# Feed-forward blocks by seven products: four products gathered in one PSUM bank, weights split two quarters at a time

## The chip, the cores and the metric

One core of a Trainium2 chip runs the whole program. Its engines are TensorE (PE, matrix products; its weight loads are shown apart as PEld), VectorE (DVE), ScalarE (ACT), GpSimd (POOL) and SyncE (SP, which here only issues DMAs). Each engine works through a list of instructions of its own, in order, and waits where an instruction needs something that another engine or a DMA has not finished. Products land in PSUM, in banks of 128x512 floats; everything else that is computed lies in SBUF.

The metric is the device time of one execution in microseconds (us). Three executions of the kernel before took 2611.4, 2611.07 and 2610.01 us, median 2611.07 us. One more was taken with the profiler: it took 2612.16 us, and its span from the first to the last instruction is 2610.0 us.

## The reference

Two layers of an encoder over 640 rows (512 new frames and 8 x 16 running ones) of width 1024. Each layer is a feed-forward block, a mixer and a second feed-forward block, and each of the six has a residual and a layer norm behind it:

```python
D_MODEL = 1024
D_FF = 2816

def swiglu(x, w_gate, w_up, w_down):
    return (jax.nn.silu(x @ w_gate) * (x @ w_up)) @ w_down

def trunk(x, states):
    for l in range(DEPTH):
        x = layer_norm(ALPHA * x + 0.5 * swiglu(x, ffn_w_gate[l, 0], ffn_w_up[l, 0], ffn_w_down[l, 0]),
                       ln_g[l, 0], ln_b[l, 0])
        ...
        x = layer_norm(ALPHA * x + m, ln_g[l, 1], ln_b[l, 1])
        x = layer_norm(ALPHA * x + 0.5 * swiglu(x, ffn_w_gate[l, 1], ffn_w_up[l, 1], ffn_w_down[l, 1]),
                       ln_g[l, 2], ln_b[l, 2])
```

The mixer `m` is a state-space model beside stick-breaking attention in layer 0 and a Mamba-2 block in layer 1. All arithmetic is in 32-bit floats.

## The kernel before

**Stages.** The program runs `ffn0`, `mix0`, `ffn1`, `ffn2`, `mix1`, `ffn3`, one behind the other; `ffn0` also carries the preparation of tables for `mix0` on its side, and `ffn3` the last state updates of `mix1` (`tick`, `side`).

**Hi and lo.** A 32-bit product is made of three products of a narrower format. Every operand is split into a rounded part hi and the rest lo: `split` (L93 to L95) makes hi with a cast on ACT (L94) and lo with a subtraction on DVE (L95). A product is then hi*hi + lo*hi + hi*lo, three matmuls per 128 rows of depth (`mm3`, L116; `product`, L336). The activations x lie split in `xhi` and `xlo`.

**Weights.** A block of weights comes by DMA as a `raw` tile of 128x1024 (four buffers, L97). It is split in pieces of 512 columns into units, tiles `w` of 128x2x512 that hold hi and lo of one piece. The pool `w` has 11 units. `load_w` (L103) loads one block and makes two units of it.

**Feed-forward.** The 2816 hidden columns are 22 blocks f of 128. Blocks 0 and 1, and the gate half of 2 and 3, are computed directly. From there on two blocks f and f+1 are taken as a pair: for the gate weights and for the up weights of a pair, the 1024x256 weight matrix is cut into four quarters a11, a12, a21, a22 of 512x128 and x into four quarters likewise, and the product is made by seven quarter products instead of eight (76 such matrices in the program: 10 up and 9 gate in each of four blocks). `operands` (L307) loads the two raw tiles r0 (a11, a12) and r1 (a21, a22), makes the sums of quarters on DVE (L319, L323) and splits seven operands A[1] to A[7]. The sums of x (`T1`, `T2`, `T4`, and one written over x) are made once for each block. `matrix` (L344) runs the products; each has 12 matmuls of 128x128 weights and 320 columns. Three PSUM banks x, y, z are used:

- products 1, then 2, in x; 6, 7 and 4 in y; 5, then 3, in z.
- ACT copies product 1 out of x (L349, `mx`). DVE adds it to product 6 (L351) and to product 5 (L353), and these two sums are added on DVE when the results are taken (L357, L359, L361).

A result of the gate goes through the silu on ACT (L371) into `s`, a tile of 128x320 for each of four results. A result of the up half is multiplied with its `s` on DVE (L377, L379) and split into the tile `h` by `finish` (L226), one 128x320 piece at a time.

**Order.** The pairs go as: gate matrix, up matrix. Before the first up matrix of every four blocks the `down` products of the four blocks before run (L396), which need four blocks of `w_down`, that is eight units, and add into `yacc` on DVE (L204). The program is written in this order, but the place of an instruction on its engine is set by a scheduler, which puts the lists together from the dependencies and its estimates; `issue_after` adds an order where it is asked for. A tile from a pool waits for the last reader of the buffer that it takes.

**Layer norm.** `load_gb` (L149) fetches gain and bias by a DMA from POOL's queue into two units of the pool `w`; `layer_norm` (L156) uses them.

Of the kernel before, what the change touches and what calls it, by code (L numbers as in the profile page):

```python
# [9 lines left out]
F32 = mybir.dt.float32  # L10
# [10 lines left out]
D = 1024  # L21
# [14 lines left out]
def kernel(ctx: ExitStack, tc: tile.TileContext, I, O, phases=PHASES):  # L36
# [9 lines left out]

    pools = {"raw": pool("raw", RAWS), "w": pool("w", UNITS)}

# [50 lines left out]

    def unit(dt=F32R, w=512):  # L100
        return pools["w"].tile([128, 1024 // w, w], dt, name="w")

    def load_w(src):  # L103

        r = raw_tile()
        nc.sync.dma_start(r, src)
        u = []
        for j in range(2):
            u.append(unit())
            split(u[j][:, 0], u[j][:, 1], r[:, 512 * j:512 * j + 512])  # L110
        return u

# [35 lines left out]

    def load_gb(n):  # L149
        g_bc = [unit(F32, D)[:, 0] for _ in range(2)]  # L150
# [3 lines left out]
        return g_bc  # L154

# [51 lines left out]
    def ffn(i, ph, last, side=None):  # L207
# [4 lines left out]
        with ExitStack() as st:  # L212
# [19 lines left out]

            def finish(f, o, L, hf):
                state["dve"] = split(ht[f][:, 0, o:o + L], ht[f][:, 1, o:o + L], hf).ins

# [15 lines left out]
            for h in range(2):  # L251
                o, L = HALVES[h]
                for f in fs:
                    pg, pu = (bank_a()[:, :L] for _ in range(2))
                    for p, u in ((pg, wg[f][0]), (pu, wg[f][1])):
                        mm3(p, [w_k(u, k) for k in range(KT)],
                            [(xh[:, k, o:o + L], xl[:, k, o:o + L]) for k in range(KT)])
                    s = wk.tile([128, 512], F32, name="sw", bufs=3)[:, :L]
                    state["silu"] = nc.scalar.activation(s, pg, AF.Silu).ins
                    V.tensor_tensor(s, pu, s, op=ALU.mult)  # L260
                    finish(f, o, L, s)
                    run_pend()
            first = {}
            for r in range(2):
                w = load_w(I["w_gate"][i, 2 + r])
                for c in range(2):
# [3 lines left out]
                    t = first[r, c] = wk.tile([128, Q], F32, name="s", bufs=4)  # L270
                    state["silu"] = nc.scalar.activation(t, p, AF.Silu).ins

# [4 lines left out]

            def minus(t, n, p, m):

                u = wk.tile([128, Q], F32, name=n, bufs=2 if n == "hf" else 4)  # L280
                V.tensor_tensor(t, quad(hf32, *p)[:, k], quad(hf32, *m)[:, k], op=ALU.subtract)
                V.tensor_tensor(u, quad(lf32, *p)[:, k], quad(lf32, *m)[:, k], op=ALU.subtract)
                V.tensor_tensor(t, t, u, op=ALU.add)

            t2, t3 = (wk.tile([128, 4, Q], F32, name="h", bufs=4) for _ in range(2))
            for k in range(4):
                t1 = wk.tile([128, Q], F32, name="mx", bufs=4)
                minus(t3[:, k], "hf", (1, 1), (0, 1))
                minus(t1, "mx", (0, 1), (0, 0))
                for part in (hf32, lf32):  # L290
# [16 lines left out]
            def operands(src0, src1):  # L307
# [3 lines left out]
                a11, a12, a21, a22 = r0[:, :512], r0[:, 512:], r1[:, :512], r1[:, 512:]  # L311
                A = {p: unit() for p in PRODUCTS}

                def part(p, v):
                    state["lo"] = split(A[p][:, 0], A[p][:, 1], v).ins

# [16 lines left out]
                part(3, s4)  # L333
                return A

# [7 lines left out]

            def matrix(A, take):  # L344

                x, y, z = (bank_a()[:, :Q] for _ in range(3))
                p1, u, v = (wk.tile([128, Q], F32, name="mx", bufs=4) for _ in range(3))
                product(x, A, 1, True)
                nc.scalar.copy(p1, x)  # L349
                product(y, A, 6, True)  # L350
                V.tensor_tensor(u, y, p1, op=ALU.add)  # L351
                product(z, A, 5, True)
                V.tensor_tensor(v, z, p1, op=ALU.add)  # L353
                product(x, A, 2, False)
                take(0, 0, x)
                product(y, A, 7, False)
                take(1, 1, lambda o: V.tensor_tensor(o, y, v, op=ALU.add))  # L357
                product(z, A, 3, False)
                take(0, 1, lambda o: V.tensor_tensor(o, z, u, op=ALU.add))  # L359
                product(y, A, 4, False)  # L360
                take(1, 0, lambda o: V.tensor_tensor(o, y, p1, op=ALU.add))  # L361

            def pair(f, before=None):
                g = first if f == 2 else {}

                def gate(r, c, v):
                    t = g[r, c] = wk.tile([128, Q], F32, name="s", bufs=4)
                    if callable(v):
                        v(t)
                        v = t  # L370
                    state["silu"] = nc.scalar.activation(t, v, AF.Silu).ins  # L371

                def up(r, c, v):
                    t = wk.tile([128, Q], F32, name="hf", bufs=2)
                    if callable(v):
                        v(t)
                        V.tensor_tensor(t, t, g[r, c], op=ALU.mult)  # L377
# [18 lines left out]
            def down(fs, norm=None):  # L396
                for f in fs:
                    wd[f] = load_w(I["w_down"][i, f])
                if norm is not None:
                    g_bc = load_gb(norm)  # L400
                for t in range(NT):
# [202 lines left out]
    def mixer0(ph, last):  # L604
# [368 lines left out]
        with ExitStack() as st:  # L973
            ctx_p.close()
            open_banks()
            for k in range(4, 8):
                wo[k] = load_w(I["m0_out"][k])
            g_bc = load_gb(LN_OF[ph])
            for t in range(NT):
# [46 lines left out]
    def mixer1(ph, last):  # L1026
# [6 lines left out]
        with ExitStack() as st:  # L1033
# [343 lines left out]
            for c in range(NT):  # L1377
                gate_out(3, c)
                if c == 0:
                    g_bc = load_gb(LN_OF[ph])  # L1380
                layer_norm(c, g_bc, last)
                if c >= 2:
                    run_pend()
# [154 lines left out]
```

## Time and profile before

| | value |
|---|---|
| median of three runs | 2611.07 us (2610.01 to 2611.4) |
| profiled execution | 2612.16 us, span 2610.0 us |
| DVE busy | 2026.8 us (78%), 4074 instructions |
| ACT busy | 1149.1 us (44%), 2400 instructions |
| POOL busy | 239.2 us (9%) |
| matmuls of the seven products (L340) | 2432 + 2736 + 1216 = 6384, 84 for each of 76 matrices |
| DMA | 302.79 MB, mean 116 GB/s |

The share of busy time of an engine is an average over six stages with different limits. An engine that is busy for 78% can still be late at one place, and an engine's idle time costs nothing where PE does not wait for it. So the table is only the start: the stages and the waits of PE decide.

### The profile page before, as it was taken

How to read it: one execution, taken by the hardware profiler on the slowest of the kernel's cores; microseconds unless marked ns; L12 is line 12 of the kernel's file. 1: busy time of each engine (PE TensorE's matmuls, PEld its weight loads, DVE VectorE, ACT ScalarE, POOL GpSimd, SP SyncE). 2: the span in 40 equal slices, each digit the busy share in tenths (PEclk: the TensorE clock that was granted, in tenths of full speed). 3: DMA queues.
4: the chain of work that ended last, by engine and by line, in shares of the span. 5: the costliest groups of instructions: out<-in, count | busy, mean ns of one | idle time of the engine just before them, and what ended most of it. 6: DMA issues, size and time to landing. Idle time of an engine off the chain costs nothing. (4 is left out here: it accounts for less than half of the span.)

```text
span 2610.0 us, 41343 instructions
## 1 busy us (share of the span) xinstructions
PE 2550.6 (98%) x15673; PEld 2311.2 (89%) x15673; DVE 2026.8 (78%) x4074; ACT 1149.1 (44%) x2400; POOL 239.2 (9%) x356
## 2 busy tenths in 40 slices
PE   9999999999879999999999999999999999999998
PEld 8999999887559999999999999889989878898887
DVE  7898888667859777768976677877786789887778
ACT  4444444346524344334433343566565553343332
POOL 0000003010020000003000001311111150000001
PEclk9999999999979999999999999999999999999999
DMA  5233234542302232222222222456564622443432
GB/s 180 97 114 99 96 110 139 175 146 84 109 24 74 81 97 98 73 85 86 75 88 81 71 91 99 128 171 195 154 208 136 217 92 94 146 151 127 132 122 93
DMA packets 165751, 302.79 MB, mean 116 GB/s; under 512 B 19072, under 2 KB 89856, under 8 KB 165040
## 3 DMA queue, kind: packets, MB, share of 16 engines
q1 hardware_dynamic: 163792, 293.83, 35.0%
q0 software_dynamic: 1760, 6.33, 0.7%
q8 instruction: 123, 2.02, 0.3%
q14 instruction: 76, 0.62, 0.1%
HBM read 259.56 MB, written 40.54 MB: 115 GB/s over the span
## 5 line engine op out<-in xcount | busy, mean ns | idle before, releaser
L127 PE MATMUL bank<-w,h 128*128 128x512 f32 x2640 | 610.9, 391 | 0.0
L127 PEld LDWEIGHTS bank<-w,h 128*128 128x128 f32 x2640 | 492.5, 188 | 105.3 <-issue 3.4
L127 PE MATMUL bank<-xhi,w 128*128 128x256 f32 (+2 forms) x2528 | 556.6, 311 | 8.8 <-ACT w L94 5.7
L95 DVE TENSOR_TENSOR w<-raw,w 128x512 fp32r<-128x512 f32 x693 | 472.0, 692 | 101.9 <-ACT w L94 99.5
L340 PE MATMUL bank<-xhi,w 128*128 128x320 f32 x2432 | 540.1, 310 | 0.7 <-DVE w L95 0.3
L94 ACT CAST w<-raw 128x512 fp32r<-128x512 f32 x693 | 422.3, 620 | 254.8 <-PE bank L340 131.0
L127 PEld LDWEIGHTS bank<-xhi,w 128*128 128x128 f32 x2528 | 421.0, 188 | 21.7 <-issue 7.2
L340 PE MATMUL bank<-T,w 128*128 128x320 f32 x2736 | 425.6, 309 | 0.1
L340 PEld LDWEIGHTS bank<-xhi,w 128*128 128x128 f32 x2432 | 406.6, 188 | 7.1 <-issue 3.9
L340 PEld LDWEIGHTS bank<-T,w 128*128 128x128 f32 x2736 | 406.6, 188 | 0.4 <-DVE w L95 0.3
L127 PE MATMUL bank<-xlo,w 128*128 128x256 f32 (+2 forms) x1264 | 391.4, 310 | 1.7 <-DVE xlo L95 1.6
L340 PE MATMUL bank<-xlo,w 128*128 128x320 f32 x1216 | 375.5, 309 | 0.0
L94 ACT CAST w<-sw 128x512 fp32r<-128x512 f32 x228 | 137.8, 620 | 457.9 <-PE bank L127 276.7
L204 DVE SCALAR_TENSOR_TENSOR yacc<-bank,yacc 128x512 f32<-128x512 f32 x240 | 164.7, 688 | 213.6 <-PE bank L127 212.0
L127 PEld LDWEIGHTS bank<-xlo,w 128*128 128x128 f32 x1264 | 238.1, 188 | 3.8 <-DVE xlo L95 2.8
L340 PEld LDWEIGHTS bank<-xlo,w 128*128 128x128 f32 x1216 | 228.2, 188 | 0.0
L95 DVE TENSOR_TENSOR w<-sw,w 128x512 fp32r<-128x512 f32 x228 | 156.1, 685 | 11.8 <-ACT w L94 11.5
L152 POOL DMA_DIRECT2D w<-in_ln_gb_dram x12 | 6.9, 576 | 1236.8 <-DVE h L95 1217.1
L127 PE MATMUL bank<-w,og 128*128 128x512 f32 x432 | 105.3, 397 | 2.2 <-DVE og L1334 2.0
L94 ACT CAST h<-hf 128x320 fp32r<-128x320 f32 x160 | 73.3, 459 | 55.9 <-DVE hf L377 48.7
L127 PEld LDWEIGHTS bank<-w,og 128*128 128x128 f32 x432 | 79.5, 188 | 20.3 <-DVE og L1334 4.2
L127 PE MATMUL bank<-w,xhi 128*128 128x512 f32 x240 | 83.3, 412 | 1.1 <-DVE yacc L779 1.1
(392 smaller groups left out, 2877.0 us busy)
## 6 DMA issues: line engine op xcount, KB each, us to landing
raw<-in_w_gate_dram SPq DMA_DIRECT2D x88, 512.0 KB, 3.7
raw<-in_w_up_dram SPq DMA_DIRECT2D x88, 512.0 KB, 3.7
raw<-in_w_down_dram SPq DMA_DIRECT2D x88, 512.0 KB, 4.1
raw<-in_m_in_dram SPq DMA_DIRECT2D x52, 512.0 KB, 3.8
raw<-in_m_out_dram SPq DMA_DIRECT2D x24, 512.0 KB, 3.8
csb<-cs_d SPq DMA_DIRECT2D x20, 512.0 KB, 5.0
h<-in_ssd_h_dram SPq DMA_DIRECT2D x16, 512.0 KB, 5.8
h<-in_ssd_h_dram SPq DMA_DIRECT2D x32, 256.0 KB, 2.7
```

The lines of the kernel that those rows point to most:

```text
L94: nc.scalar.copy(hi, src)
L95: return nc.vector.tensor_tensor(lo, src, hi.bitcast(F32), op=ALU.subtract)
L127: state["pe"] = nc.tensor.matmul(ps, a, b, start=(k == 0), stop=(k == n - 1)).ins
L152: nc.gpsimd.dma_start(g_bc[j], bass.AP(tensor=I["ln_gb"].tensor, offset=I["ln_gb"].offset + (2 * n + j) * D, ap=[[0, 128], [1, D]]))
L204: state["acc"] = nc.vector.scalar_tensor_tensor(ya, pb, scale, ya, op0=ALU.mult, op1=ALU.add).ins
L340: nc.tensor.matmul(ps, A[p][:, a, k * 128:k * 128 + 128], B[p][b][:, k, :], start=(first and n == 0), stop=(n == 11), skip_group_check=True)
```

## The change

- **Products.** The order 1, 6, 5, 2, 7, 3, 4 becomes 1, 2, 6, 5, 7, 3, 4. Products 1, 6, 7 and 4 are all gathered in bank x, 5 and 3 in w, and 2 alone in z. The sums on the way are copied out by ACT (`keep`): product 1 from x, 1+6 from x, 5 from w. DVE's two additions into `mx` (L351, L353) go; the results are one addition each, and the last one is read from the bank.
- **Splits.** A tile of the pool `w` now holds two pieces (128x2x2x512); there are 5 of them, and one single unit in a pool `w1`. One cast and one subtraction split 1024 columns (`split2`). For this the sums of quarters are written so that two operands that are needed together lie side by side: (1, 2) in r0 as it comes, (6, 5) in `sums`, (7, 3) written over r0; A[4] goes into `w1`.
- **Rows.** `s` and `hf` become tiles of 640 columns, so that the first block of a pair is multiplied and split 640 columns at a time and the second is split so.
- **Layer norm.** Gain and bias no longer take units of `w`: they go into T1 and T2, into a small pool of their own, or into h0.

```diff
-UNITS = 11
-PRODUCTS = (1, 6, 5, 2, 7, 3, 4)
+PAIRS = 5
...
-    pools = {"raw": pool("raw", RAWS), "w": pool("w", UNITS)}
+    pools = {"raw": pool("raw", RAWS), "w": pool("w", PAIRS), "w1": pool("w1", 1)}
...
-    def unit(dt=F32R, w=512):
-        return pools["w"].tile([128, 1024 // w, w], dt, name="w")
+    def unit():
+        return pools["w1"].tile([128, 2, 512], F32R, name="w1")
+
+    def two_units():
+        return pools["w"].tile([128, 2, 2, 512], F32R, name="w")
+
+    def split2(w, src):
+
+        return split(w[:, :, 0], w[:, :, 1], src.rearrange("p (j c) -> p j c", j=2))
 
     def load_w(src):
 
         r = raw_tile()
         nc.sync.dma_start(r, src)
-        u = []
-        for j in range(2):
-            u.append(unit())
-            split(u[j][:, 0], u[j][:, 1], r[:, 512 * j:512 * j + 512])
-        return u
+        w = two_units()
+        split2(w, r)
+        return w[:, 0], w[:, 1]
...
-                s1, s2, s4 = (wk.tile([128, 512], F32, name="sw", bufs=3) for _ in range(3))
-                V.tensor_tensor(s1, a21, a22, op=ALU.add)
-                part(1, a11)
-                total(s2, s1, a11, ALU.subtract)
-                part(4, a22)
-                total(a21, a11, a21, ALU.subtract)
-                part(6, s2)
-                total(s4, a12, s2, ALU.subtract)
-                part(5, s1)
-                part(2, a12)
-                part(7, a21)
-                part(3, s4)
+                u, v, w = (two_units() for _ in range(3))
+                sums = wk.tile([128, 1024], F32, name="sw", bufs=1)
+                s2, s1 = sums[:, :512], sums[:, 512:]
+                part(u, r0, 1, 2)
+                total(s1, a21, a22, ALU.add)
+                total(s2, s1, a11, ALU.subtract)
+                part(v, sums, 6, 5)
+                total(a12, a12, s2, ALU.subtract)
+                total(a11, a11, a21, ALU.subtract)
+                part(w, r0, 7, 3)
+                A[4] = unit()
+                split(A[4][:, 0], A[4][:, 1], a22)
                 return A
...
-                x, y, z = (bank_a()[:, :Q] for _ in range(3))
-                p1, u, v = (wk.tile([128, Q], F32, name="mx", bufs=4) for _ in range(3))
-                product(x, A, 1, True)
-                nc.scalar.copy(p1, x)
-                product(y, A, 6, True)
-                V.tensor_tensor(u, y, p1, op=ALU.add)
-                product(z, A, 5, True)
-                V.tensor_tensor(v, z, p1, op=ALU.add)
-                product(x, A, 2, False)
-                take(0, 0, x)
-                product(y, A, 7, False)
-                take(1, 1, lambda o: V.tensor_tensor(o, y, v, op=ALU.add))
-                product(z, A, 3, False)
-                take(0, 1, lambda o: V.tensor_tensor(o, z, u, op=ALU.add))
-                product(y, A, 4, False)
-                take(1, 0, lambda o: V.tensor_tensor(o, y, p1, op=ALU.add))
+                x, w, z = (bank_a()[:, :Q] for _ in range(3))
+                e = {}
+
+                def keep(n, ps):
+                    e[n] = wk.tile([128, Q], F32, name="mx", bufs=3)
+                    nc.scalar.copy(e[n], ps)
+
+
+                product(x, A, 1, True)
+                keep(1, x)
+                product(z, A, 2, True)
+                take(0, 0, z, e[1])
+                product(x, A, 6, False)
+                keep(2, x)
+                product(w, A, 5, True)
+                keep(5, w)
+                product(x, A, 7, False)
+                take(1, 1, x, e[5])
+                product(w, A, 3, False)
+                take(0, 1, w, e[2])
+                product(x, A, 4, False)
+                take(1, 0, x, None)
...
+                def up(r, c, ps, e):
+                    c = slice(Q * c, Q * c + Q)
+                    t = row(f + r)
+                    if e is not None:
+                        V.tensor_tensor(t[:, c], ps, e, op=ALU.add)
+                        ps = t[:, c]
+                    if r == 0:
+                        if c.start:
+                            V.tensor_tensor(t, t, g[0], op=ALU.mult)
+                            finish(f)
                     else:
-                        V.tensor_tensor(t, v, g[r, c], op=ALU.mult)
-                    finish(f + r, Q * c, Q, t)
+                        V.tensor_tensor(t[:, c], ps, g[1][:, c], op=ALU.mult)
+                        if not c.start:
+                            finish(f + 1)
```

What this does to the lists of the engines is shown for one gate matrix of `ffn1`, the second of the first four blocks. PE first, around products 6 and 5: `bank_8642` is x, `bank_8643` y and `bank_8644` z. Before:

```order
L340 MATMUL bank_8642<-xhi_79,w_8614 128x320 x2
L340 MATMUL bank_8642<-xlo_80,w_8614 128x320
L340 MATMUL bank_8643<-T2_8280,w_8615 128x320 x12
L340 MATMUL bank_8644<-T1_8279,w_8616 128x320 x12
L340 MATMUL bank_8642<-xhi_79,w_8617 128x320 x2
```

And now, where `bank_8129` is x, `bank_8130` w and `bank_8131` z:

```order
L353 MATMUL bank_8131<-xhi_82,w_8112 128x320 x2
L353 MATMUL bank_8131<-xlo_83,w_8112 128x320
L353 MATMUL bank_8129<-T2_7802,w_8113 128x320 x12
L353 MATMUL bank_8130<-T1_7801,w_8113 128x320 x12
L353 MATMUL bank_8129<-xhi_82,w_8114 128x320 x2
L353 MATMUL bank_8129<-xlo_83,w_8114 128x320
```

Before, two products (6 and 5) lie between the end of product 1 in x and the next product in that bank; now one product lies between any two in bank x, and ACT's copy, or DVE's read, has to be done in that time.

On ACT, the same matrix before (`w_8615` to `w_8619` are its own operands, `w_8750` to `w_8755` those of the next, `h` the pieces of the up matrix ahead):

```order
L94 CAST h_8496<-hf_8588 128x320
L349 COPY mx_8645<-bank_8642 128x320
L94 CAST h_8497<-hf_8605 128x320
L94 CAST w_8751<-sw_8758 128x512
L94 CAST w_8752<-sw_8757 128x512
L94 CAST w_8753<-raw_8746 128x512
L371 ACTIVATE s_8699<-bank_8642 128x320
L94 CAST w_8754<-raw_8747 128x512
L94 CAST w_8755<-sw_8759 128x512
```

And now (`mx_8144`, `mx_8173` and `mx_8187` are the copies of 1, of 1+6 and of 5; `w1_8126` is its own A[4], `w_8235` to `w_8237` are the next matrix's pairs):

```order
L93 CAST w1_8126<-raw_8109 128x512
L364 COPY mx_8144<-bank_8129 128x320
L93 CAST w_8235<-raw_8231 128x2x512
L392 ACTIVATE s_8158<-s_8158 128x320
L364 COPY mx_8173<-bank_8129 128x320
L364 COPY mx_8187<-bank_8130 128x320
L93 CAST w_8236<-sw_8238 128x2x512
L392 ACTIVATE s_8201<-s_8201 128x320
```

The cast of the pair `w_8236` now stands behind the copy of product 5.

On DVE, before, from the sum with product 5 to the result that product 7 completes (`s_8713`):

```order
L353 TENSOR_TENSOR mx_8647<-bank_8644,mx_8645 128x320
L95 TENSOR_TENSOR w_8756<-raw_8747,w_8756 128x512
L319 TENSOR_TENSOR raw_8747<-raw_8746,raw_8747 128x512
L95 TENSOR_TENSOR w_8751<-sw_8758,w_8751 128x512
L319 TENSOR_TENSOR sw_8759<-raw_8746,sw_8758 128x512
L95 TENSOR_TENSOR w_8752<-sw_8757,w_8752 128x512
L357 TENSOR_TENSOR s_8713<-bank_8643,mx_8647 128x320
```

And now, up to the same result (`s_8201`, from bank x, before product 4 may go into it):

```order
L390 TENSOR_TENSOR s_8158<-bank_8131,mx_8144 128x320
L94 TENSOR_TENSOR w_8235<-raw_8231,w_8235 128x2x512
L332 TENSOR_TENSOR sw_8238<-raw_8232 128x512
L332 TENSOR_TENSOR sw_8238<-sw_8238,raw_8231 128x512
L94 TENSOR_TENSOR w_8236<-sw_8238,w_8236 128x2x512
L390 TENSOR_TENSOR s_8201<-bank_8129,mx_8187 128x320
```

The result now stands directly behind the subtraction of 1024 columns for `w_8236`, which itself needs the cast that stands behind the copy of product 5. Of the 76 matrices 42 have this order.

More of the change, by code (lines that the diff above doesn't have):

```diff
@@ L147, in run_pend, with load_gb @@
             pend.pop(0)()
-    def load_gb(n):
-        g_bc = [unit(F32, D)[:, 0] for _ in range(2)]
+    def load_gb(n, g_bc):
         for j in range(2):
@@ L311, in operands, with part @@
                 a11, a12, a21, a22 = r0[:, :512], r0[:, 512:], r1[:, :512], r1[:, 512:]
-                A = {p: unit() for p in PRODUCTS}
-                def part(p, v):
-                    state["lo"] = split(A[p][:, 0], A[p][:, 1], v).ins
+                A = {}
+                def part(w, src, *ps):
+                    for n, p in enumerate(ps):
+                        A[p] = w[:, n]
+                    state["lo"] = split2(w, src).ins
                 def total(o, v, w, op):
@@ L363, in pair, with gate @@
             def pair(f, before=None):
                 g = first if f == 2 else {}
[L366 to L377, printed above, removed]
-                    else:
-                        V.tensor_tensor(t, v, g[r, c], op=ALU.mult)
-                    finish(f + r, Q * c, Q, t)
+                def gate(r, c, ps, e):
+                    if r not in g:
+                        g[r] = g_row()
+                    t = g[r][:, Q * c:Q * c + Q]
+                    if e is not None:
+                        V.tensor_tensor(t, ps, e, op=ALU.add)
+                        ps = t
+                    state["silu"] = nc.scalar.activation(t, ps, AF.Silu).ins
@@ L977, in mixer0 @@
                 wo[k] = load_w(I["m0_out"][k])
-            g_bc = load_gb(LN_OF[ph])
+            gb = pool("m0_gb", 1, st, reuse_waits="tile")
+            g_bc = [gb.tile([128, D], F32, name=f"gb{n}") for n in range(2)]
+            load_gb(LN_OF[ph], g_bc)
             for t in range(NT):
@@ L1379, in mixer1 @@
                 if c == 0:
-                    g_bc = load_gb(LN_OF[ph])
+                    g_bc = [wk.tile([128, 2, 512], F32, name="h0", bufs=4).rearrange("p a b -> p (a b)")
+                            for _ in range(2)]
+                    load_gb(LN_OF[ph], g_bc)
                 layer_norm(c, g_bc, last)
```

34 lines of the change are left out of this document (21 added, 13 removed).

## Prediction

> **What bounds the kernel now.** First the page: its busy times, then the granted clock.
>
> ```profile
> span 2610.0 us, 41343 instructions
> PE 2550.6 (98%) x15673; PEld 2311.2 (89%) x15673; DVE 2026.8 (78%) x4074; ACT 1149.1 (44%) x2400; POOL 239.2 (9%) x356
> PEclk9999999999979999999999999999999999999999
> ```
>
> PE is busy for 98%, at full clock but for one slice. Busy time of pipelined matmuls is modelled, so the next look is at the stages (busy time in windows; the number behind the window is its length): `ffn0`, `mix0`, `ffn1`, `ffn2`, `mix1`, `ffn3`.
>
> ```profile
> 160.00:450.00 290.00, 288.59 (x1724) 267.18 (x1724) 245.94 (x548) 126.94 (x251) 25.61 (x31) 1.00 0.36 116
> 470.00:790.00 320.00, 290.25 (x1973) 230.27 (x1972) 217.52 (x436) 149.33 (x261) 35.02 (x60) 0.95 0.31 99
> 820.00:1220.00 400.00, 400.00 (x2387) 373.69 (x2386) 297.19 (x536) 158.67 (x294) 22.78 (x19) 1.00 0.26 85
> 1230.00:1640.00 410.00, 410.00 (x2433) 384.23 (x2433) 307.36 (x568) 163.21 (x307) 14.14 (x13) 1.00 0.25 82
> 1650.00:2160.00 510.00, 500.90 (x3263) 449.18 (x3262) 390.44 (x869) 287.61 (x779) 106.59 (x199) 1.00 0.54 166
> 2180.00:2560.00 380.00, 379.71 (x2184) 342.67 (x2183) 306.05 (x551) 140.17 (x271) 0.00 (x0) 1.00 0.40 129
> ```
>
> In the four feed-forward windows PE idles 1.41 + 0 + 0 + 0.29 = 1.7 us in 1480. It idles 29.8 us in `mix0` and 9.1 in `mix1`. The waits of PE say the same; L340 is the line of the seven products:
>
> ```profile
> PE bank L853 <- ACT S L82: 10.2, 9, 5.1
> PE bank L897 <- ACT es L82: 8.6, 4, 4.5
> PE bank L340 <- DVE w L95: 0.3, 1, 0.3
> PE bank L340 <- ACT mx L349: 0.2, 1, 0.2
> ```
>
> Whether busy is also at full pace is read from the timeline inside a matrix of `ffn1` (start, length):
>
> ```profile
> 918.62 3.68 PE L340 MATMUL bank<-T,w 128*128 128x320 f32 x24
> 922.13 0.45 PE L340 MATMUL bank<-xhi,w 128*128 128x320 f32 x2
> ```
>
> 24 matmuls start within 922.13 - 918.62 = 3.51 us: 0.146 us each, **1.755 us for a product of 12**, 12.3 us for a matrix of 84. So in the feed-forward blocks nothing but the matmuls themselves takes time, and there is almost no wait that a lighter DVE or ACT could shorten.
>
> **The change part by part.** *Matmuls.* 84 per matrix before and after, the same sizes and as many weight loads: 0 us.
>
> *DVE and ACT work.* The groups of the page and of the list by form (count, busy us, mean ns):
>
> ```profile
> L95 DVE TENSOR_TENSOR w<-raw,w 128x512 fp32r<-128x512 f32 x693 | 472.0, 692 | 101.9 <-ACT w L94 99.5
> L94 ACT CAST w<-raw 128x512 fp32r<-128x512 f32 x693 | 422.3, 620 | 254.8 <-PE bank L340 131.0
> L94 ACT CAST w<-sw 128x512 fp32r<-128x512 f32 x228 | 137.8, 620 | 457.9 <-PE bank L127 276.7
> L95 DVE TENSOR_TENSOR w<-sw,w 128x512 fp32r<-128x512 f32 x228 | 156.1, 685 | 11.8 <-ACT w L94 11.5
> L353 DVE TENSOR_TENSOR mx<-bank,mx 128x320 f32<-128x320 f32 x76 | 37.0, 487 | 5.8 <-PE bank L340 5.6
> L351 DVE TENSOR_TENSOR mx<-bank,mx 128x320 f32<-128x320 f32 x76 | 36.9, 486 | 3.2 <-PE bank L340 1.2
> L349 ACT COPY mx<-bank 128x320 f32<-128x320 f32 x76 | 32.3, 426 | 57.3 <-PE bank L340 56.0
> ```
>
> Some 920 splits of 512 become 422 of 1024 and 76 of 512. The trace has no split of 1024; it has both operations at 768 and others at 1024:
>
> ```profile
> 15.21 0.84 ACT L94 CAST xhi<-raw 128x768 fp32r<-128x768 f32 x1
> 16.38 0.95 DVE L95 TENSOR_TENSOR xlo<-raw,xhi 128x768 fp32r<-128x768 f32 x1
> L1217 ACT ACTIVATE csb<-csb 128x1024 f32<-128x1024 f32 x20 | 21.2, 1058 | 21.9 <-DVE csb L1215 11.9 <-DVE rms L1328 7.6 <-PE bank L127 2.5
> L1223 DVE TENSOR_TENSOR csb<-csb,cbm 128x1024 f32<-128x1024 f32 x20 | 24.7, 1234 | 0.2
> ```
>
> From 512 to 768 the cast grows by 0.22 us and the subtraction by 0.26, so I estimate 1.06 and 1.22 us at 1024, next to the 1.06 and 1.23 of the last two rows. DVE's splits then take 422 x 1.22 + 76 x 0.69 = 567 us in place of 628 (-61), and L351 and L353 go (-74). ACT saves 560 - 422 x 1.06 - 76 x 0.62 = 66 us and pays 152 more copies x 0.426 = 65. So DVE gets some 135 us lighter or more (the 640-wide rows add a little) and ACT stays. **None of it is on the path in the feed-forward blocks**: PE hides it all, 0 us. What it is worth in the mixers, where only `load_w` changes, is a rival below.
>
> *New waits.* Here the change can cost. Before, between product 1 and the next product in x lay two products, 3.51 us; now every two products in x have one between them, 1.755 us, in which ACT must copy. Product 1 ends 0.19 us before ACT's copy starts (918.62 above, 918.81 here), and the next ACT instruction starts 0.32 us after the copy did:
>
> ```profile
> 918.81 0.43 ACT L349 COPY mx<-bank 128x320 f32<-128x320 f32 x1
> 919.13 0.63 ACT L94 CAST w<-raw 128x512 fp32r<-128x512 f32 x1
> ```
>
> A copy alone is done 0.62 us after its product, well inside 1.755. What is queued with it matters. ACT to DVE, DVE to DVE, and ACT to a waiting PE:
>
> ```profile
> 912.35 0.62 ACT L94 CAST w<-sw 128x512 fp32r<-128x512 f32 x1 [21.38 <-PE bank L127]
> 913.00 0.69 DVE L95 TENSOR_TENSOR w<-sw,w 128x512 fp32r<-128x512 f32 x1 [0.70 <-ACT w L94]
> ...
> 918.58 0.68 DVE L319 TENSOR_TENSOR raw<-raw 128x512 f32<-128x512 f32 x1
> 919.18 0.68 DVE L95 TENSOR_TENSOR w<-sw,w 128x512 fp32r<-128x512 f32 x1
> ...
> 2226.84 0.42 ACT L349 COPY mx<-bank 128x320 f32<-128x320 f32 x1 [1.76 <-PE bank L340]
> ...
> 2227.32 0.41 PE L340 MATMUL bank<-xhi,w 128*128 128x320 f32 x1 [0.22 <-ACT mx L349]
> 2227.57 1.62 PE L340 MATMUL bank<-T,w 128*128 128x320 f32 x10
> ```
>
> DVE starts 0.03 us after ACT's end; a DVE instruction starts 0.08 before the end of the one ahead; PE restarts 0.06 after ACT's end, and the matmul behind it comes after 0.25 instead of 0.146, so a stall costs its length and 0.10 more.
>
> **The tightest chain**, in the 42 matrices with the order shown above: end of product 5, copy of 5, cast of 1024 for the next matrix, its subtraction, then the result 1+6+7 read from x, and only then product 4 into x. From the end of product 5: 0.19 + 0.32 + 1.06 + 0.03 + (1.22 - 0.08) + 0.49 + 0.06 = **3.29 us**. PE comes to product 4 after products 7 and 3, 3.51 us. It fits by 0.22 us: 0 us, but with nothing to spare. The other gaps are wider. In the 36 gate matrices behind an up matrix, the copy of product 1 waits for that matrix's last result (a multiplication, then a 640-wide and a 512-wide cast). From the end of product 4, without backlog: 0.19 + 0.49 + 0.03 + about 0.7 + 0.5 + 0.4 + 0.06 = 2.4 us of the 3.51 before product 6. The single unit of `w1` is released by product 4 of one matrix and needed by product 4 of the next, 10.5 us later. The five pairs come free in the order of use (after 2, after 5, after 3), and during `down` one pair is free, enough for products 1 and 2 of the matrix behind it (3.51 us), while the four of `w_down` come free within the last 12 matmuls.
>
> *Start.* The first matmul waits for a cast of 1024 instead of 512 (+0.44 us), but stops afterwards for x anyway, at 8.07 and 8.79 us; 0 us, at most +0.5.
>
> **Sum**: 0 against the execution's own 2612.16 us, which lies 1.1 us over the median of 2611.07. I forecast **2612 us**. A difference under 0.2%, 5.2 us, can hardly be told from none.
>
> [...]
>
> **Rivals.** *1. The tight chain does not fit: slower.* Pairs of 512 do not always pack:
>
> ```profile
> 913.03 1.30 ACT L94 CAST w<-raw 128x512 fp32r<-128x512 f32 x2
> 913.69 1.37 DVE L95 TENSOR_TENSOR w<-raw,w 128x512 fp32r<-128x512 f32 x2
> ```
>
> If a whole split took as long as these, the chain would be 3.29 + 0.24 + 0.15 = 3.68 us: 0.17 late and 0.10 for the restart, 0.27 x 42 = 11 us, **2623**. It decides from 0.22 us over my sum. For it: so little room, and the scheduler fills the room with its own estimates. Against it: four rows agree on 1.06 and 1.22, and PE waited for nothing of the kind before. [...]
>
> *2. The mixers gain: faster.* PE waits there, and its clock falls at the end of the attention:
>
> ```profile
> 700.00:720.00 20.00, 14.79 (x90) 8.99 (x89) 18.63 (x28) 12.43 (x20) 1.17 (x2) 0.98 0.66 210
> 720.00:740.00 20.00, 10.43 (x58) 6.75 (x56) 6.99 (x9) 4.97 (x8) 0.00 (x0) 0.50 0.09 26
> ```
>
> At 700 to 720 DVE is full. A block's split costs DVE 2 x 0.69 - 1.22 = 0.16 us less; 26 blocks in `mix0` give 4 us, 56 in `mix1` 9. If half of the 13 us shortens PE's waits: **2605**. Against it: few of these splits stand in the serial end, where after 720 DVE is idle two thirds of the time.
>
> *3. The lists of the mixers come out worse.* The scheduler orders them anew; if the 39 us of waits grow by a fifth, **2620**.
>
> *4. It does not do what it says.* Then DVE's busy time stays near 2027, and the time too; it is inside the forecast.
>
> **How the numbers follow.** Forecast (2606 to 2617) 0.60, rival 1 0.20, rival 3 0.08, rival 2 0.12. So faster 0.12, same 0.60, slower 0.28. The range takes rival 2's 2605 and rival 1's 2623: **2604 to 2624**.
>
> **What would show it.** Right: PE's idle in the four windows stays under 5 us, 84 matmuls of 0.146 us, DVE near 1890 us or less, ACT near 1150. Wrong by rival 1: waits of PE's product line for DVE's `s` and `hf`, dozens of them at 0.1 to 0.3 us. Wrong by 2 or 3: another sum of waits on `S`, `es` or `og`. What would upset the forecast altogether is a wait of microseconds in each matrix, such as PE for `w1` or for a pair.

## The result, and the profile after

The changed kernel took 2646.04 us (median of four runs, 2641.96 to 2650.0), the kernel before 2611.24 (four runs): ratio 1.0133, 95% interval 1.0115 to 1.015. It is slower by 35 us, and the forecast range ended at 2624. From the page of the changed kernel:

```profile
span 2644.1 us, 40071 instructions
PE 2559.6 (97%) x15673; PEld 2315.7 (88%) x15673; DVE 1914.1 (72%) x3380; ACT 1118.3 (42%) x2050; POOL 248.8 (9%) x356
```

DVE is 113 us lighter, ACT 31, and the span is 34.1 us longer. PE's busy time grew by 9.0 us (2559.6 - 2550.6) with the same 15673 matmuls, its idle time by 25.1 (84.5 - 59.4). Where? The stages again, with edges set to the start of the same matmuls in both traces (the counts behind PE agree within what the trace loses). First before: `ffn0`, `mix0`, `ffn1` with `ffn2`, `mix1`, `ffn3`.

```profile
6.00:448.00 442.00, 439.92 (x2641) 410.72 (x2642) 379.84 (x871) 193.27 (x381) 32.56 (x33) 1.00 0.36 118
448.00:826.00 378.00, 347.39 (x2361) 285.68 (x2360) 270.54 (x547) 177.55 (x319) 45.52 (x71) 0.95 0.33 105
826.00:1646.00 820.00, 819.70 (x4885) 766.34 (x4884) 616.43 (x1123) 327.56 (x609) 41.83 (x36) 1.00 0.26 84
1646.00:2169.00 523.00, 510.88 (x3331) 458.21 (x3330) 403.42 (x895) 295.22 (x794) 109.90 (x203) 1.00 0.54 166
2169.00:2601.00 432.00, 431.71 (x2460) 389.69 (x2459) 350.38 (x631) 152.67 (x297) 7.11 (x6) 1.00 0.37 122
```

The same work in the changed kernel (window, its length, then PE, PEld, DVE, ACT, POOL, the granted clock, DMA):

```profile
6.00:456.00 450.00, 442.82 (x2641) 412.96 (x2642) 359.01 (x717) 190.00 (x313) 31.68 (x32) 0.99 0.35 117
456.00:838.00 382.00, 348.80 (x2365) 286.07 (x2364) 266.74 (x510) 171.50 (x285) 48.65 (x72) 0.95 0.32 103
838.00:1657.00 819.00, 818.57 (x4880) 765.58 (x4879) 560.66 (x830) 314.76 (x482) 42.15 (x35) 1.00 0.26 84
1657.00:2203.00 546.00, 517.13 (x3333) 461.13 (x3332) 395.14 (x831) 287.06 (x734) 116.86 (x203) 0.98 0.51 157
2203.00:2635.00 432.00, 431.97 (x2463) 389.93 (x2461) 327.14 (x487) 152.21 (x236) 7.11 (x6) 1.00 0.38 124
```

`ffn1` with `ffn2`, where 38 of the 76 matrices run, take 819 us as before, though DVE has 56 us less to do there. The loss stands in the other stages: 8 us in `ffn0`, 4 in `mix0`, **23 in `mix1`**, a stage whose code the change hardly touches. Of these 23, 16.7 are idle time of PE (28.9 against 12.1) and 6.3 slower matmuls: the granted clock falls to 0.98. The waits of PE (us in total, times, longest) say for whom:

```profile
PE bank L131 <- ACT w L93: 14.2, 5, 6.3
PE bank L131 <- DVE w L94: 7.0, 6, 2.3
PE bank L353 <- ACT w L93: 2.6, 1, 2.6
```

It is mostly not the product line L353 that waits, but L131, the ordinary products, for the split of a weight block. (The longest, 6.3 us, is the first load of all.) Before, the same two waits, on what was then L127, were small but for that first load:

```profile
PE bank L127 <- ACT w L94: 5.7, 1, 5.7
PE bank L127 <- DVE w L95: 1.1, 2, 0.9
```

In `mix1` alone the two come to 8.0 and 3.3 us now, before to 0 and 1.1; the rest of PE's new idle time there lies in smaller waits.

The longest new stall, in the timeline of PE, ACT, DVE and SP of the changed kernel (start, length; what follows the idle time in brackets is what ended it):

```profile
1977.96 0.33 SPq L112 DMA_DIRECT2D raw<-in_m_in_dram  x1
...
1984.52 0.34 PE L131 MATMUL bank<-xlo,w 128*128 128x384 f32 x1
...
1984.89 0.37 ACT L1119 COPY ext<-bank 128x256 f32<-128x256 f32 x1 [2.67 <-PE bank L131]
...
1987.11 0.38 PE L1357 MATMUL bank<-ones,zz 128*128 128x2 f32 x2
...
1990.86 1.07 ACT L93 CAST w<-raw 128x1024 fp32r<-128x1024 f32 x1
1991.98 0.90 PE L131 MATMUL bank<-xhi,w 128*128 128x256 f32 x2 [4.49 <-ACT w L93]
...
1993.88 0.69 DVE L1352 TENSOR_TENSOR yb<-yb,zz 128x512 f32<-128x512 f32 x1 [2.81 <-DMA zz<-z_d]
1994.49 1.22 DVE L94 TENSOR_TENSOR w<-raw,w 128x1024 fp32r<-128x1024 f32 x1
1995.76 0.58 PE L131 MATMUL bank<-xhi,w 128*128 128x256 f32 x1 [2.03 <-DVE w L94]
```

The raw weights of a block of m1_in are ordered at 1977.96. ACT is idle for 2.67 us ahead of 1984.89, and yet the cast of the block comes only behind the last read of the block before (PE, 1984.52), and then behind all that ACT has to do for the same chunk: 4.49 us of PE's time. DVE's half stands behind an instruction that waits for a DMA: 2.03 more. A smaller case of the same shape. ACT is idle for 1.60 us ahead of the last read of the block before, and then works on that chunk's results first:

```profile
1865.57 0.34 PE L131 MATMUL bank<-xlo,w 128*128 128x384 f32 x1
...
1865.94 0.37 ACT L1119 COPY ext<-bank 128x256 f32<-128x256 f32 x1 [1.60 <-PE bank L131]
...
1867.47 1.04 ACT L93 CAST w<-raw 128x1024 fp32r<-128x1024 f32 x1
...
1868.56 0.57 PE L131 MATMUL bank<-xhi,w 128*128 128x256 f32 x2 [1.31 <-ACT w L93]
```

Last read of one block, then cast of the next, then PE: this looks like single buffering (one place for a block, which is not filled before it has been read). The code says why it could be so. In `mix1`, `gate_out` keeps four blocks of m1_out for a whole group of five chunks:

```python
wo[g] = [load_w(I["m1_out"][4 * g + k]) for k in range(4)]
```

Before, these take 8 of 11 units, and three are left to a block of m1_in (two units) and half of the next. Now they take four of five pairs. The eleventh unit has become `w1`, which the blocks of m1_in do not use, and **one** pair is left. This is the theory that the experiments had to test against others.

### The profile page after: what moved, and what is told of

Same layout as the page of the kernel before. It is cut to its first block, busy times and chain, and to the rows that moved or that the text cites. A ratio compares the mean times of both kernels' runs of the same rounds, so it can differ in the third digit from the quotient of the medians.

```text
span 2644.1 us, 40071 instructions
## 1 busy us (share of the span) xinstructions
PE 2559.6 (97%) x15673; PEld 2315.7 (88%) x15673; DVE 1914.1 (72%) x3380; ACT 1118.3 (42%) x2050; POOL 248.8 (9%) x356
## 5 line engine op out<-in xcount | busy, mean ns | idle before, releaser
L131 PE MATMUL bank<-w,h 128*128 128x512 f32 x2640 | 612.1, 392 | 2.3 <-DVE w L94 2.3
L131 PEld LDWEIGHTS bank<-w,h 128*128 128x128 f32 x2640 | 493.5, 188 | 107.9 <-issue 3.4
L131 PE MATMUL bank<-xhi,w 128*128 128x256 f32 (+2 forms) x2528 | 560.7, 313 | 20.3 <-ACT w L93 14.2
L94 DVE TENSOR_TENSOR w<-raw,w 128x1024 fp32r<-128x1024 f32 (+1 forms) x423 | 476.4, 1136 | 121.5 <-ACT w L93 120.1
L353 PE MATMUL bank<-xhi,w 128*128 128x320 f32 x2432 | 539.6, 310 | 0.0
L93 ACT CAST w<-raw 128x1024 fp32r<-128x1024 f32 (+1 forms) x423 | 401.5, 970 | 180.0 <-DVE raw L332 81.6
L131 PEld LDWEIGHTS bank<-xhi,w 128*128 128x128 f32 x2528 | 424.0, 189 | 35.3 <-ACT w L93 15.6
L353 PE MATMUL bank<-T,w 128*128 128x320 f32 x2736 | 427.9, 310 | 3.5 <-ACT w L93 2.6
L353 PEld LDWEIGHTS bank<-T,w 128*128 128x128 f32 x2736 | 408.1, 188 | 5.3 <-ACT w L93 2.8
L353 PEld LDWEIGHTS bank<-xhi,w 128*128 128x128 f32 x2432 | 406.6, 188 | 5.5 <-issue 3.9
L131 PE MATMUL bank<-xlo,w 128*128 128x256 f32 (+2 forms) x1264 | 391.9, 311 | 1.2 <-DVE xlo L94 1.2
L353 PE MATMUL bank<-xlo,w 128*128 128x320 f32 x1216 | 375.5, 309 | 0.0
L93 ACT CAST w<-sw 128x1024 fp32r<-128x1024 f32 x76 | 79.8, 1050 | 399.1 <-PE bank L131 270.3
L131 PEld LDWEIGHTS bank<-xlo,w 128*128 128x128 f32 x1264 | 239.5, 190 | 3.5 <-DVE xlo L94 1.7
L353 PEld LDWEIGHTS bank<-xlo,w 128*128 128x128 f32 x1216 | 228.2, 188 | 0.5 <-issue 0.5
L364 ACT COPY mx<-bank 128x320 f32<-128x320 f32 x228 | 96.6, 423 | 174.7 <-PE bank L353 174.2
L94 DVE TENSOR_TENSOR w<-sw,w 128x1024 fp32r<-128x1024 f32 x76 | 93.0, 1224 | 62.2 <-ACT w L93 61.8
L131 PE MATMUL bank<-w,og 128*128 128x512 f32 x432 | 106.6, 399 | 2.5 <-ACT og L1364 2.0
L131 PEld LDWEIGHTS bank<-w,og 128*128 128x128 f32 x432 | 81.0, 191 | 20.8 <-DVE og L1365 2.7
L1141 DVE SCALAR_TENSOR_TENSOR acc<-ext,cw,acc 128x512 f32<-128x512 f32 (+1 forms) x144 | 68.9, 546 | 29.8 <-POOL cvo L1131 16.7
```

The costliest lines, as they stand in the source:

```text
L93: nc.scalar.copy(hi, src)
L94: return nc.vector.tensor_tensor(lo, src, hi.bitcast(F32), op=ALU.subtract)
L131: state["pe"] = nc.tensor.matmul(ps, a, b, start=(k == 0), stop=(k == n - 1)).ins
L353: nc.tensor.matmul(ps, A[p][:, a, k * 128:k * 128 + 128], B[p][b][:, k, :], start=(first and n == 0), stop=(n == 11), skip_group_check=True)
L364: nc.scalar.copy(e[n], ps)
L1141: V.scalar_tensor_tensor(o_, i_, cw[:, m, w:w + 1], o_, op0=ALU.mult, op1=ALU.add)
```

## The experiments

The runs of the kernel before beside them had medians of 2610.35 to 2612.34 us. The table gives for each run what its profiled execution took more than that of the kernel before between the same matmuls, in us; the edges are the starts of matmuls 0, 2640, 5000, 9880, 13210 and the last in the order of time. Each row is one execution; the first and last us, outside these edges, hold another 1.0 us of the changed kernel's 34.1.

| run | median | ratio, 95% interval | ffn0 | mix0 | ffn1, ffn2 | mix1 | ffn3 |
|---|---|---|---|---|---|---|---|
| changed | 2646.04 | 1.0133 (1.0115 to 1.015) | 7.6 | 3.5 | -0.3 | 22.8 | -0.5 |
| e1 narrow | 2633.64 | 1.0086 (1.0071 to 1.0101) | 0.3 | 2.4 | 0.8 | 17.1 | -1.0 |
| e2 narrow in load_w | 2637.08 | 1.0103 (1.0087 to 1.012) | 5.2 | 2.0 | 0.8 | 17.1 | -0.5 |
| e3 narrow in operands | 2637.96 | 1.0103 (1.0088 to 1.0118) | 3.2 | 5.1 | -0.5 | 16.2 | -1.1 |
| e4 gain, bias in a pair | 2651.25 | 1.0152 (1.0137 to 1.0167) | 6.6 | 6.8 | 4.1 | 21.7 | -0.6 |
| e5 more room in mix1 | 2621.71 | 1.0045 (1.003 to 1.006) | 5.8 | 7.2 | -0.3 | -4.1 | -0.2 |
| e6 both e1 and e5 | 2612.77 | 1.0008 (0.9999 to 1.0017) | 1.4 | 2.4 | 0.8 | -5.7 | -1.0 |
| e7 before, 10 units | 2625.16 | 1.0058 (1.0041 to 1.0075) | 4.2 | 3.0 | 1.1 | 4.5 | 0.1 |
| e8 before, gathered | 2611.25 | 1.0001 (0.9992 to 1.0011) | -1.5 | 0.6 | -0.7 | 1.7 | -0.2 |
| e9 before, gain and bias | 2610.61 | 0.9998 (0.9989 to 1.0007) | -0.8 | 0.2 | -0.6 | -1.1 | 0.0 |
| e10 e9, 12 units in mix1 | 2617.83 | 1.0023 (1.0014 to 1.0033) | -0.3 | 1.9 | -0.7 | 3.2 | 0.0 |
| e11 e10, later | 2614.23 | 1.0009 (1.0001 to 1.0018) | -2.4 | 1.8 | -0.6 | 2.1 | -0.1 |
| e12 e8 and e11 | 2610.89 | 0.9999 (0.999 to 1.0008) | -2.5 | 1.0 | -0.4 | 0.5 | 0.0 |

How far can one execution be trusted? Where two kernels have the same instructions in the same order on PE, ACT, DVE and POOL in a stage (the traces leave out buffer numbers), what their executions differ by there is hardly the code: in `mix1` 0.1 us (e1, e2), 1.6 (e11, e12), 1.7 (before, e8) and 6.6 (changed, e3), in `mix0` up to 3.7 (changed, e5). So a difference of a few us in one cell shows nothing by itself; the medians and what repeats in several runs do.

**Width of the splits (e1 to e3).** All wide splits, those of `load_w`, or those of the operands, done as two of 512 each:

```diff
-        return split(w[:, :, 0], w[:, :, 1], src.rearrange("p (j c) -> p j c", j=2))
+        for j in range(2):
+            r = split(w[:, j, 0], w[:, j, 1], src[:, 512 * j:512 * j + 512])
+        return r
```

> The changed kernel with each wide split done as two splits of 512 (one half after the other, into the same pair tile). All else as changed: the gathered products, 5 pairs and one single unit, gain and bias elsewhere. Changed kernel 2646, before 2611; of the 33 us between the profiled spans 8 arise in ffn0, 3 in mix0, 23 in mix1, none in ffn1, ffn2, ffn3. Theory A (the wide split is late: one cast of 1.06 and one subtraction of 1.22 us have to find room in the lists of ACT and DVE as whole pieces, and PE waits for the whole): most of the loss goes, 2611 to 2620. Theory B (five pairs, each released only when both its halves are read, feed the mixers later than 11 units did): no gain, 2640 to 2650. Theory C (any change of the splits makes the scheduler write the mixers' lists anew, and those happen to be worse): some other number, 2615 to 2650, with other places of loss than the changed kernel.

> The changed kernel with two splits of 512 in load_w alone (the mixers' weights, w_down, and the blocks computed directly); the operands of the seven products keep the wide splits. Theory A: the mixers' 26 us and the 4 us at w_down in ffn0 go, the other 4 us of ffn0 (a product waiting for its operand at 161 us) stay: 2612 to 2622. Theory B: 2640 to 2650. Theory C: 2615 to 2650, other places.

> The changed kernel with two splits of 512 for the operands of the seven products alone; load_w keeps the wide split. Theory A: only the 4 us at 161 us of ffn0 go, the mixers keep their loss: 2640 to 2646. Theory B: 2640 to 2650. Theory C: the lists of the mixers hold nothing of these operands, but what ffn0 and ffn3 carry beside them may move: 2635 to 2650.

Theory A fails as the whole cause: with every split narrow 22 us are left, and 17 of them in `mix1`. But the width has a part, since e1 is 12 us under the changed kernel. The two halves gain 9 and 8 us alone; with intervals of some 4 us to either side, no run tells whether they add. None of the three medians lies in a range of theory A or B. All lie in theory C's, but theory C fails for `mix1`: the loss stays at the same places. The stalls ahead of a block of m1_in stay in e1: 4.2, 1.5 and 3.8 us. Around them (matmuls 11260 to 11300, 11650 to 11720, 11980 to 12020) the changed kernel loses 3.4, 6.1 and 9.2 us, 18.7 of its 22.8, and e1 7.7, 5.9 and 6.2.

The 6.6 us that e3 spends less in `mix1` do not come from lists written anew either, since the lists there are those of the changed kernel. PE's idle time is nearly the same (27.0 us for 28.9), but PE ran at half clock for 10.2 us where it was 20.5 in the changed kernel's execution; the last section comes back to this.

**Gain and bias (e4)**, put back into the pool as one pair:

```diff
+    def gb_tiles():
+        t = pools["w"].tile([128, 2, D], F32, name="w")
+        return [t[:, 0], t[:, 1]]
```

> The changed kernel with gain and bias of the layer norm in one pair tile again, as before the change they took two units of the same pool. Theory A and theory C (for these tiles): they touch only the ends of the six stages, 2640 to 2650. Rival D: the new places (T1 and T2, a small pool, h0) make the layer norm or the work ahead of it wait, and bring the loss at the end of mix1 and of mix0: 2636 or less.

Rival D falls: the new places are no loss; without them the median is 5 us higher, just above the range given. Beside the changed kernel, e4 loses 2 to 4 us at the end of each of `mix0`, `ffn1`, `ffn2` and `mix1`, where one pair fewer is left.

**Room in mix1 (e5, e6).** From the sixth on, every second block of m1_in goes into `w1` and one new unit:

```diff
+            def load_in(src):
+                nin.append(0)
+                if len(nin) < 5 or len(nin) % 2:
+                    return load_w(src)
...
+                w = (unit(), wk.tile([128, 2, 512], F32R, name="w2"))
+                for j in range(2):
+                    split(w[j][:, 0], w[j][:, 1], r[:, 512 * j:512 * j + 512])
+                return w
```

> The changed kernel, in mix1 alone with room for one more block of weights: every second block of m1_in from the fifth on goes into the single unit w1 (idle there) and a new unit of its own, by two splits of 512, the others into pairs as changed; to make room cbm has one buffer for two and e8 lies in the buffer of ecs. Theory B2 (what is left of B after the narrow splits, whose 2634 still lose 16 us in mix1: m1_out of a group holds four of the five pairs while the group is worked off, so that the next block of m1_in cannot be split before the one before it has been read; 11 units left three): the three stalls ahead of a block of m1_in (matmuls 11275, 11692 and 12004) go, mix1 loses under 8 instead of 23 us: 2625 to 2634. Theory C (lists written anew, no matter how many buffers): stalls of the same size at these or other places, 2640 to 2655.

> The same room in mix1, and all splits of 512 as in the first experiment (2634). Theory B2: 2612 to 2621. Theory C: 2628 to 2640.

With wide splits left everywhere else, room alone turns `mix1` from 22.8 us over the kernel before into 4.1 under it, and the run takes 24 us less, 3 below the range given. At the three places nothing is lost any more (0.0, -0.6 and 0.0 us, in e6 too). `mix1` in e5:

```profile
1659.00:2178.00 519.00, 508.97 (x3332) 457.02 (x3332) 398.32 (x849) 289.19 (x752) 120.72 (x203) 1.00 0.53 165
```

PE's idle time is 10 us for 28.9, the clock full again. The place of the long stall, first PE, then the last casts of weights on ACT ahead of it:

```profile
1976.16 1.09 PE L1315 MATMUL bank<-csb,xd 128*64 128x128 f32 x16
1977.18 0.50 PE L131 MATMUL bank<-xhi,w 128*128 128x256 f32 x2
```

```profile
1960.30 0.61 ACT L93 CAST w<-raw 128x512 fp32r<-128x512 f32 x1
...
1963.43 0.62 ACT L93 CAST w<-raw 128x512 fp32r<-128x512 f32 x1
```

The block is ready some 13 us ahead and PE goes straight on. e6 has room and narrow splits and is within 0.2% of the kernel before: the two account for the loss, and the 640-wide rows, which e6 keeps and no run tried alone, cost nothing that shows.

**One unit fewer, single units (e7):** `UNITS = 10` in the kernel before.

> The kernel before with 10 units in place of 11, nothing else changed: the amount of room that the mixers have in the changed kernel, still by single units of 512. Theory B2: the stalls ahead of a block of m1_in arise here too, at the same three matmuls: 2617 to 2632. Theory A alone (width of the splits): 2610 to 2614. Theory C: anything from 2608 to 2630, at other places.

The time fits theory B2 (+15 us), the places do not. None of the three stalls ahead of m1_in is there (the three places lose 0.6, 1.6 and 0.4 us), and `mix1` loses 4.5 us instead of 17 in e1, which has 10 units too, but in pairs. So the larger part of the loss in `mix1` goes with the pairs. The reason, from the code: with single units a half of the next block can be made as soon as one unit is free, and a unit is free as soon as its half is read. (e1 and e7 also differ in products, rows and gain and bias; of these, products and gain and bias cost nothing in e8 and e9, and the rows are in the feed-forward code alone.) The missing unit costs in other places, the largest of them in `ffn0`, in the matrix where a product also waits 2.6 us in the changed kernel:

```profile
159.24 1.17 PE L340 MATMUL bank<-T,w 128*128 128x320 f32 x3 [3.22 <-DVE w L95]
```

**The other edits alone, in the kernel before (e8, e9).** e8 has the new `matrix` with its three copies and the order 1, 2, 6, 5, 7, 3, 4; e9 has the new tiles for gain and bias:

```diff
-                    g_bc = load_gb(norm)
+                    g_bc = [wk.tile([128, 2, 4, Q], F32, name=f"T{n}", bufs=1).rearrange("p a k c -> p (a k c)")[:, :D]
+                            for n in (1, 2)]
+                    load_gb(norm, g_bc)
```

> The kernel before with the new order of products, the gathering of 1, 6, 7 and 4 in one bank and the three copies, alone; units, splits of 512 and 320-wide rows as before. My prediction held the gathering to be free, and DVE some 74 us lighter: 2608 to 2614. If the gathering has a part in the loss: 2615 or more, with waits of PE's product line.

> The kernel before (11 units, splits of 512, old products) with only the gain and bias of the layer norm moved as in the change (T1 and T2, a small pool, h0). By the narrow runs the end of mix1 gets 4.5 us shorter with these tiles (matmuls 13000 to 13210), since they no longer take units that the next blocks of weights need. If that is their doing: 2605 to 2609, with the 4 us in that stretch. If it came from the splits: 2609 to 2612.

Both are free. The 4.5 us at the end of `mix1` that I hoped to see again in e9 did not come back: between matmuls 13000 and 13210 e9 loses 0.8 us. It gains 2.4 just ahead of them (12850 to 13000), but so does e7 (2.3), whose gain and bias are where they were.

**More than eleven units (e10 to e12).** Every third half block of m1_in in a twelfth unit, at once (e10) or from the ninth half block on (e11); e12 is e11 with the products of e8. The lines of e11 (e10 has no `len(nin) < 9`):

```diff
+            def in_unit():
+                nin.append(0)
+                return unit() if len(nin) < 9 or len(nin) % 3 else wk.tile([128, 2, 512], F32R, name="w2")
```

> The same, and one more unit of 4 KB in mix1 alone (12 units), taken by every third half block of m1_in. If room in mix1 is still what PE waits for at 11 units: 2 to 6 us less than the run beside it, 2600 to 2607. If 11 units are enough there (PE idles for only 9 us in mix1 before, little of it ahead of m1_in): the same as the run beside it within 2 us.

> As the run before (the kernel before, gain and bias moved, one more unit in mix1), but the new unit is taken only from the ninth half block of m1_in on, since the run before lost its 5 us in the first blocks of mix1 (matmuls 9880 to 10900), where six half blocks are under way at once. If those 5 us came from the single new buffer being asked for twice there: 2607 to 2611, none of it there. If they came from lists written anew: 2612 to 2620. That twelve units beat eleven elsewhere in mix1: 2605 or less.

> The same with the gathered products, in the old units and splits: all of the changed kernel that is not the pair tile. By the single runs each part is free: 2605 to 2611. Nothing in the traces says that it should lie clearly under the kernel before, since PE has 98% there.

A twelfth unit gains nothing. e10 misses both of its ranges and loses 5.5 us in the first blocks of `mix1` (matmuls 9880 to 10900). Taking the unit later, e11 loses 2.2 there and 2.5 right behind (10900 to 11260); e12, with the same lists in `mix1`, loses 0.2 and 2.2. So the loss in the first blocks is smaller without the early use, and whether the second is the new buffer or the lists is not settled. Eleven units are enough where they are units, and no run beats the kernel before: e12 takes 2610.89 with the gathered products and the moved gain and bias (without the 640-wide rows and the pair tile).

## Why the prediction was wrong

**The feed-forward steps were right, but for `ffn0`.** *Gathering is free*: e8, and 819 us for `ffn1` with `ffn2`. *The tight chain fits*: in an up matrix of `ffn1` product 5 ends with the 24 matmuls of 6 and 5, and product 4 starts at 939.03 (changed kernel, PE, ACT, DVE):

```profile
932.00 3.68 PE L353 MATMUL bank<-T,w 128*128 128x320 f32 x24
935.51 0.45 PE L353 MATMUL bank<-xhi,w 128*128 128x320 f32 x2
...
935.71 0.43 ACT L364 COPY mx<-bank 128x320 f32<-128x320 f32 x1 [1.28 <-PE bank L353]
936.07 1.05 ACT L93 CAST w<-sw 128x1024 fp32r<-128x1024 f32 x1
...
937.15 1.22 DVE L94 TENSOR_TENSOR w<-sw,w 128x1024 fp32r<-128x1024 f32 x1 [1.17 <-ACT w L93]
938.30 0.48 DVE L398 TENSOR_TENSOR hf<-bank,mx 128x320 f32<-128x320 f32 x1
...
939.03 0.45 PE L353 MATMUL bank<-T,w 128*128 128x320 f32 x2
```

938.30 + 0.48 + 0.06 - 935.51 = 3.33 us against 3.29 forecast; it fits by 0.19 where 0.22 was forecast. In none of the 76 matrices does PE idle for more than 0.02 us ahead of product 4. Rival 1 did not happen.

**The width of 1024** was sized well (1.05 and 1.24 us for 1.06 and 1.22), what it saves was not: DVE lost 113 us of busy time, not 135 or more. Added up by their lengths DVE's instructions did lose 158 us. The sum took lengths, which overlap. In DVE's timeline an instruction starts before the one ahead has ended:

```profile
927.73 1.23 DVE L94 TENSOR_TENSOR w<-sw,w 128x1024 fp32r<-128x1024 f32 x1 [1.08 <-ACT w L93]
928.87 0.68 DVE L206 SCALAR_TENSOR_TENSOR yacc<-bank,yacc 128x512 f32<-128x512 f32 x1
929.47 0.68 DVE L332 TENSOR_TENSOR raw<-raw,sw 128x512 f32<-128x512 f32 x1
930.07 0.68 DVE L332 TENSOR_TENSOR raw<-raw 128x512 f32<-128x512 f32 x1
```

1.14 us from a wide one to the next, 0.60 from a narrow one: by starts, two narrow ones cost 2 x 0.60 - 1.14 = 0.06 us more, not 2 x 0.69 - 1.22 = 0.16. By the lengths measured here it is 2 x 0.69 - 1.24 = 0.14 us. ACT, which was to stay, lost 31 us of busy time: its casts of weights took some 76 us less for the 66 forecast, and its casts of `h` 18 less by the 640-wide rows, which the sum left out.

**The step that failed** is the room for weights. The prediction counted it for the feed-forward blocks alone ("The five pairs come free in the order of use") and held that in the mixers "only `load_w` changes", worth 0.16 us of DVE a block. It did not count what the mixers hold at a time. Four of five pairs are bound in `mix1`, and one pair cannot be filled while it is read; 11 units, taken and released one by one, left three. The price is the 23 us of `mix1` and, with the width, a part of the 11 us of `ffn0` and `mix0`. e5 shows the room in `mix1`, e7 beside e1 the pairs; in `mix0` the room was not changed alone.

A second step failed in `ffn0`: that PE hides the wider splits, "0 us". PE waits there for the wide pieces themselves, at the first `down` and at one operand of a product (4.2 and 4.3 us lost in the changed kernel, matmuls 200 to 350 and 850 to 950). At the second e7, with narrow pieces and one unit fewer, loses 4.4, so the missing unit has a part there too.

**The rivals.** Rival 3 (the mixers' lists come out worse) had the place and the sign, at 2620 and a chance of 0.08. Its price, a fifth of the old 39 us of waits, was a guess without a mechanism. The waits that were to show it, on `S` and `es`, hardly moved (11.7 and 8.1 us for 10.2 and 8.6); the ones on `w` grew. It also left out what follows a stall: I charged 0.10 us for a restart, but at the end of the 4.49 us stall of `mix1` the clock was at half from 1991.4 to 2001.6, for 10.2 us. In all, PE's busy time rose by 9.0 us for the same matmuls, a quarter of the loss. Rival 2 (the lighter DVE gains in the mixers) came out only where there was room: `mix1` in e5 and e6 lies 4 to 6 us under the kernel before, which may as well be the room or, in part, the execution.

**The grain of the splits** had a part of its own. With room in `mix1`, narrow splits are worth 9 us (e5 to e6), in `ffn0` and `mix0`. At the two places in `ffn0`, e2 (narrow in `load_w`) loses 1.0 and 4.2 us, e3 (narrow operands) 1.5 and 2.7, e1 (both) 0.5 and 1.5. The first is the first `down`: DVE is full with the sums of x (busy for 5.81 of the 6 us from 50 to 56), and PE waits for a wide subtraction behind them. From the changed kernel:

```profile
53.75 0.48 DVE L312 TENSOR_TENSOR h<-h,xlo 128x320 f32<-128x320 f32 x1
54.15 1.21 DVE L94 TENSOR_TENSOR w<-raw,w 128x1024 fp32r<-128x1024 f32 x1
...
55.42 1.11 PE L131 MATMUL bank<-w,h 128*128 128x512 f32 x3 [2.34 <-DVE w L94]
```

In e1 this stall is gone. It is 0.97 us in e5, which has the wide splits too and differs in `ffn0` by the place of one instruction, so its size is not the width alone. How much of the 9 us is the width itself and how much the lists that come out differently with it, no run tells apart.

## What to carry to other kernels

A pool that several stages share is to be counted in each of them: how many pieces are held at the peak, how many are left, and in what grain they come free. Joining two pieces into one tile takes the half piece away that kept the next load going, and the price stands in a stage that the diff hardly touches. Joining two subtractions on DVE, which was not the bound here, saved 0.06 us by the distance of starts, while going back to narrow pieces gained 9 us (e5 to e6). And before a cause is read from a few us of one stage, it helps to see how far two executions with the same lists in that stage lie apart (up to 6.6 us here).

## What the hardware showed

PE's granted clock fell behind one stall and not behind a longer one. Windows of the changed kernel behind the 2.34 us stall at 53.08, and behind one of 2.85 us:

```profile
56.00:60.00 4.00, 4.00 (x12) 3.18 (x11) 3.39 (x7) 0.00 (x0) 0.00 (x0) 0.57 0.43 131
```

```profile
1661.49 1.09 PE L193 MATMUL bank<-ident,yacc 128*128 128x128 f32 x8 [2.85 <-POOL yacc L176]
...
1662.00:1666.00 4.00, 3.96 (x36) 3.79 (x35) 3.92 (x8) 1.72 (x4) 3.68 (x8) 1.00 0.63 208
```

The first is followed by a clock of 0.57 in the 4 us behind it, the second by 1.00. So the length of a stall alone did not decide it here; what did, the traces do not settle. In `mix1` of the changed kernel PE ran at half clock in four stretches, from 1824.2, 1936.8, 1991.4 and 2134.8 on, 20.5 us in all, and e3 with the same lists there for 10.2 us. So the same lists took different times, 6.6 us apart.

At the long stall of `mix1` the two waits of 4.49 and 2.03 us cost more behind them:

```profile
1992.00:1998.00 6.00, 3.97 (x14) 3.25 (x15) 4.07 (x10) 0.85 (x2) 2.06 (x4) 0.50 0.70 230
1998.00:2004.00 6.00, 6.00 (x31) 6.00 (x30) 0.00 (x0) 1.43 (x2) 0.00 (x0) 0.69 0.08 31
```
